# Weight sums ahead of the raw split, and seven-product pairs at places 1, 4 and 6, in a hybrid decoder layer

## The chip, the cores and the metric

The kernel runs on one core of a Trainium2 chip. The metric is the device time of one launch in microseconds (us), the median of several runs. Engines are named as in the profile: PE multiplies matrices (PEld is its weight load), DVE is the vector engine, ACT the scalar engine, POOL is GpSimd, and SP issues the DMAs of this kernel.

## The reference

One decoder layer for 256 tokens of width 2048 in float32: half a SwiGLU FFN, a token mixer of two head groups, and half an FFN again. Only the two FFNs are touched by the change.

```python
def swiglu(x, w_gate, w_up, w_down):
    return (jax.nn.silu(x @ w_gate) * (x @ w_up)) @ w_down

x = x + 0.5 * swiglu(rms_norm(x, ffn1_norm[l]), ffn1_w_gate[l], ffn1_w_up[l], ffn1_w_down[l])
...  # projection, attention, output projection
x = x + 0.5 * swiglu(rms_norm(x, ffn2_norm[l]), ffn2_w_gate[l], ffn2_w_up[l], ffn2_w_down[l])
```

`w_gate` and `w_up` are 2048 x 5632, `w_down` is 5632 x 2048.

## The kernel before

**Precision.** Each float32 operand is split into two parts, `hi` (a cast on ACT) and `lo` (the difference, on DVE), by `split`. A product is three matmuls of 128x512: hi by hi (L478), lo of x by hi of w (L479), hi of x by lo of w (L480).

**Pairs and blocks.** The width of an FFN, 5632, is cut into 11 chunks of 512. For a chunk, gate and up are computed together as a block product (`pair`); the down projection of one part (chunks 0 to 3, 4 to 7, 8 to 10) is computed for two column chunks at a time in the same way (`down`). Both call `blocks`, which goes over 8 places j (6 in the down projections of the last part). At each place a raw tile of 4 x 512 columns (`w_raw`, 1 MB, two DMAs) is loaded and multiplied. A **plain** place takes eight products (24 matmuls): its raw tile is cast whole (`w_hi`, `w_lo`, 128x2048). A **seven** place takes seven products by Strassen's scheme (21 matmuls): three quarters of the raw tile are split (128x1536), four sums of weights `w_t` are formed on DVE (L461, L463, L464) and split too (`t_hi`, `t_lo`). Which places are sevens is in `STRASSEN`; the last place is never one. Products are added up in PSUM banks m1 to m7. m1, m6 and m7 get products from sevens alone, so after the last seven place three operations (L487 to L489) turn them into `s1`, `v` and `u`, and at the end of the sequence more DVE operations put these together with m2 to m5.

There are 30 such sequences: 14 in FFN 1 (its first chunk and its last down projection are plain linear products) and 16 in FFN 2.

**Left-hand sides.** A seven needs other sums of x than a plain place: `Stage.put_sums` makes them for x, and `to_gT` for the activations g of a pair: two places per chunk, each with four transposes (L379), a copy, sums, and splits.

**Buffers and order.** `w_raw` has three buffers, `w_hi` and `w_lo` have two, `w_t`, `t_hi` and `t_lo` one. The four banks of one sequence's m2 to m5 are the other four for the next one (`banks.swap`): m2, m4 and m5 of the next sequence take the banks of m1, m6 and m7. The order in which each engine gets its instructions is set by a scheduler that reorders the program; an engine then executes its own list in that order, and a waiting instruction holds what is behind it.

Of the kernel before, what the change touches and what calls it, by code (L numbers as in the profile page):

```python
# [25 lines left out]
CH = 512  # L26
NCH = D_FF // CH
FF_PARTS = [(0, 4), (4, 8), (8, 11)]
STRASSEN = (1, 3, 5)
PAD_C, PAD_S, PAD_X = 256, 320, 224  # L30
CMP_BLOCK = 32
CMP_STRIDE = 16
# [13 lines left out]
def hybrid_layer(ctx: ExitStack, tc: tile.TileContext, d: dict, out: bass.AP):  # L46
# [146 lines left out]
    def split(hi, lo, src):  # L193
        cast = nc.scalar.copy(hi, src)  # L194
        nc.vector.tensor_tensor(lo, src, hi.bitcast(F32), op=ALU.subtract)  # L195
        return cast
# [40 lines left out]
    newest = {}  # L237
# [113 lines left out]
    def ffn(st, wg, wu, wd, after, fpool, last_part, plain_end, groups=None):  # L351
# [2 lines left out]
        wuv = wu.rearrange("(k p) n -> p k n", p=P)  # L354
        wdv = wd.rearrange("(k p) n -> p k n", p=P)

        def to_gT(slot, sg, odd, sums):


            yield from wait(2)  # L360
            hi = gpool.tile([P, 8, P], F32R, tag=f"ghi{slot}", name="ghi")
            lo = gpool.tile([P, 8, P], F32R, tag=f"glo{slot}", name="glo")
            xhi = fpool.tile([P, 5, P], F32R, tag=f"gxhi{slot}", name="gxhi")
            xlo = fpool.tile([P, 5, P], F32R, tag=f"gxlo{slot}", name="gxlo")

            def put(x, o, n, src):
                h, l = ((hi, lo), (xhi, xlo))[x]
                split(h[:, o:o + n], l[:, o:o + n], src)

            def where(x, o):  # L370
                h, l = ((hi, lo), (xhi, xlo))[x]
                return h[:, o], l[:, o]

            for i in range(2):
                seven = i == 1 and odd
                pt = misc("gt").rearrange("p (a b) -> p a b", b=P)
                order = ((0, 1), (0, 0), (1, 0), (1, 1)) if seven else ((0, 0), (0, 1), (1, 0), (1, 1))
                for n, (j, t) in enumerate(order):
                    nc.tensor.transpose(pt[:, n], sg[t][:, (2 * i + j) * P:(2 * i + j + 1) * P], ident)  # L379
                if not sums:  # L380
                    put(0, 4 * i, 4, pt)
                    g[2 * slot + i] = [where(0, 4 * i + f) for f in range(4)]
                    yield False
                    continue
                gf = fpool.tile([P, 8, P], F32, tag="sv", name="gf")
                nc.scalar.copy(gf[:, :4], pt)
                if seven:
                    put(1, 0, 3, pt[:, 1:])

                    nc.vector.tensor_tensor(gf[:, 4], gf[:, 0], gf[:, 1], op=ALU.subtract)  # L390
                    nc.vector.tensor_tensor(gf[:, 5:7], gf[:, 0:5:4], gf[:, 3:4].to_broadcast([P, 2, P]), op=ALU.add)
                    nc.vector.tensor_tensor(gf[:, 7], gf[:, 2], gf[:, 6], op=ALU.subtract)
                    put(0, 4, 4, gf[:, 4:])
                    g[2 * slot + 1] = {A11: where(1, 0), A12: where(1, 1), A22: where(1, 2), NS3: where(0, 4),
                                       S1: where(0, 5), S2: where(0, 6), S4: where(0, 7)}
                else:
                    put(0, 4 * i, 4, pt)
                    nc.vector.tensor_tensor(gf[:, 4:6], gf[:, 0:3:2], gf[:, 1:4:2], op=ALU.subtract)
                    o = 0 if i else 3
                    put(1, o, 2, gf[:, 4:6])  # L400
                    g[2 * slot + i] = {A11: where(0, 4 * i), A21: where(0, 4 * i + 1), A12: where(0, 4 * i + 2),
                                       A22: where(0, 4 * i + 3), S3: where(1, o), DD: where(1, o + 1)}
                yield False
# [30 lines left out]
        def blocks(nj, sevens, form, load, middle):  # L434

            pm = {i: acc(f"m{i}") for i in (2, 4, 5, 3)}
            side = banks.side
            banks.free = side[3:]  # L440
            seen = set()
            last = {}
            plan = []
            for j in range(nj):
                if j in sevens:

                    plan.append([(1, A11, 1), (2, A12, 2), (3, S4, 3), (5, S1, 4), (7, NS3, 5), (6, S2, 6), (4, A22, 7)])
                else:
                    plan.append([(2, A11, 1), (2, A12, 2), (4, A21, 1), (4, A22, 2), (5, A21, 0), (5, A22, 3),
                                 (3, S3, 0), (3, DD, 3)])  # L450
                for i, (m, _, _) in enumerate(plan[-1]):
                    last[m] = (j, i)
            for j in range(nj):
                raw = wpool.tile([P, 4, CH], F32, tag="raw", bufs=3, name="w_raw")
                newest["load"] = load(j, raw)
                whi = wpool.tile([P, 4, CH], F32R, tag="whi", name="w_hi")
                wlo = wpool.tile([P, 4, CH], F32R, tag="wlo", name="w_lo")
                if j in sevens:
                    newest["cast"] = split(whi[:, 1:4], wlo[:, 1:4], raw[:, 1:4])
                    ts = fpool.tile([P, 4, CH], F32, tag="ts", name="w_t")  # L460
                    nc.vector.tensor_tensor(ts[:, 0:2], raw[:, 0:1].to_broadcast([P, 2, CH]), raw[:, 1:4:2],  # L461
                                            op=ALU.subtract)
                    nc.vector.tensor_tensor(ts[:, 2], raw[:, 3], ts[:, 0], op=ALU.subtract)  # L463
                    nc.vector.tensor_tensor(ts[:, 3], raw[:, 2], ts[:, 2], op=ALU.subtract)  # L464
                    thi = fpool.tile([P, 4, CH], F32R, tag="thi", name="t_hi")
                    tlo = fpool.tile([P, 4, CH], F32R, tag="tlo", name="t_lo")
                    split(thi, tlo, ts)
                    for m in (1, 6, 7):
                        if m not in pm:
                            pm[m] = banks.tile(side[(1, 6, 7).index(m)], f"m{m}")  # L470
                else:
                    newest["cast"] = split(whi, wlo, raw)
                for i, (m, f, s) in enumerate(plan[j]):
                    ahi, alo = form(j, f)
                    bhi, blo = (whi[:, s], wlo[:, s]) if s < 4 else (thi[:, s - 4], tlo[:, s - 4])
                    first, end = m not in seen, last[m] == (j, i)
                    seen.add(m)
                    nc.tensor.matmul(pm[m], ahi, bhi, start=first, stop=False)  # L478
                    nc.tensor.matmul(pm[m], alo, bhi, start=False, stop=False)  # L479
                    nc.tensor.matmul(pm[m], ahi, blo, start=False, stop=end)  # L480
                    if i % 2 == 1:
                        pump()
                if j == max(sevens):

                    sv = fpool.tile([P, 2, CH], F32, tag="sv", name="sv")
                    s1, v, u = sv[:, 0], sv[:, 1], ev("u")
                    nc.scalar.copy(s1, pm[1])  # L487
                    nc.vector.tensor_tensor(v, pm[6], s1, op=ALU.add)
                    nc.vector.tensor_tensor(u, pm[7], v, op=ALU.add)  # L489
                    middle(s1, v, u)  # L490
            return pm, s1, v, u
# [26 lines left out]
        def down(k0, nj, ca, cb, ready):  # L518


            def load(j, raw):
                rows = slice(k0 + 2 * j, k0 + 2 * j + 2)
                nc.sync.dma_start(raw[:, 0:4:3], wdv[:, rows, cb * CH:(cb + 1) * CH])
                return nc.sync.dma_start(raw[:, 1:3], wdv[:, rows, ca * CH:(ca + 1) * CH]).ins

            def add(t, c, x):
                nc.vector.scalar_tensor_tensor(xr[t][c], x, 0.5, xr[t][c], op0=ALU.mult, op1=ALU.add)

            def middle(s1, v, u):
                add(0, ca, s1)  # L530
                add(0, cb, v)
                add(1, ca, u)
                add(1, cb, u)

            pm, s1, v, u = blocks(nj, [j for j in STRASSEN if j < nj - 1], gform, load, middle)
            add(0, ca, pm[2])
            add(1, ca, pm[4])
            if ready:
                ready(ca)
            add(0, cb, pm[5])  # L540
            add(1, cb, pm[5])
            add(0, cb, pm[3])
            banks.swap()
            if ready:
                ready(cb)

        for pi, (c0, c1) in enumerate(FF_PARTS):
# [4 lines left out]
            for c in range(c0, c1):  # L552
                sg = pair(c) if c else plain_pair(c)
                i = c - c0
                spawn(to_gT(i, sg, not plain and 2 * i + 1 in STRASSEN and 2 * i + 1 < nj - 1, not plain))
            if final:
                last_part()
            if not plain:
# [588 lines left out]
```

## Time and profile before

| | us |
|---|---|
| runs, median (lowest to highest of 3) | 1871.52 (1871.22 to 1871.9) |
| the profiled execution's own time | 1872.38 |
| its span | 1870.7 |
| PE busy | 1840.8 (98%) |
| PEld busy | 1509.9 (81%) |
| DVE busy | 1485.6 (79%) |
| ACT busy | 968.7 (52%) |

The busy time of PE is modelled, as matmuls overlap: a matmul of 128x512 is drawn 0.39 us long, and the next one may start 0.23 us after it. Idle time of an engine is listed with what ended it, which the profile infers from semaphores. Time of the engines other than the one at the bound costs nothing by itself.

### The profile page before, as it was taken

The numbers are of one execution on the slowest core, as the hardware profiler recorded it, in microseconds if no ns is written. First come the engines' busy times: TensorE is split into PE (matmuls) and PEld (weight loads), VectorE is DVE, ScalarE is ACT, GpSimd is POOL, SyncE is SP. The second block draws the span as 40 slices with busy tenths as digits, with TensorE's granted clock in tenths as the row PEclk, the third lists the DMA queues.
The fourth block names the chain that finished last, engine by engine and source line by source line (L and its number), as shares of the span: only waits on it lengthen the run. The fifth ranks groups of instructions, "written<-read, shape, count | busy, mean of one in ns | idle before, by whom it ended". The sixth has DMA issues, their size and how long they took to land.

```text
span 1870.7 us, 22225 instructions
## 1 busy us (share of the span) xinstructions
PE 1840.8 (98%) x8542; PEld 1509.9 (81%) x8542; DVE 1485.6 (79%) x1619; ACT 968.7 (52%) x1018; POOL 3.9 (0%) x22
## 2 busy tenths in 40 slices
PE   8999999999999999999999999999999999999998
PEld 6887788777788778788888888888788777788777
DVE  7888888888888875666655567788888888988887
ACT  7555444555454445335455555555544555545553
POOL 0000000000000000000000000000000000000000
PEclk9999999999999999999999999999999999999999
DMA  8655565655666655764533445655556555566554
GB/s 310 204 184 180 187 217 187 202 197 182 201 219 196 207 178 201 243 212 146 164 118 114 155 159 180 203 193 189 186 198 214 190 181 199 184 213 201 194 183 155
DMA packets 190762, 356.65 MB, mean 191 GB/s; under 512 B 10528, under 2 KB 25792, under 8 KB 190656
## 3 DMA queue, kind: packets, MB, share of 16 engines
q1 hardware_dynamic: 188912, 354.65, 57.3%
q8 instruction: 67, 1.10, 0.2%
q10 hardware_dynamic: 1744, 0.58, 0.1%
q14 instruction: 39, 0.32, 0.1%
HBM read 353.09 MB, written 2.10 MB: 190 GB/s over the span
## 4 chain that ended last, share of the span: by engine, by line
PE 93%; ACT 3%; DVE 2%; issue 1%; DMA 1%; SPq 0%; DVEq 0%; ACTq 0%
PE m L480 21%; PE m L478 21%; PE m L479 21%; PE in L258 4%; PE in L256 4%; PE in L257 4%; ACT t_hi L194 2%; PE wo L256 1%; PE wo L258 1%; PE wo L257 1%; PE down L258 1%; PE down L257 1%; PE down L256 1%; PE gt L379 1%; DVE w_lo L195 1%
## 5 line engine op out<-in xcount | busy, mean ns | idle before, releaser
L195 DVE TENSOR_TENSOR w_lo<-w_raw,w_hi 128x1536 fp32r<-128x1536 f32 (+3 forms) x331 | 694.0, 2101 | 209.9 <-ACT w_hi L194 195.5
L194 ACT CAST w_hi<-w_raw 128x1536 fp32r<-128x1536 f32 (+3 forms) x331 | 577.4, 1761 | 543.1 <-PE m L479 345.0
L478 PE MATMUL m<-w_hi,xhi 128*128 128x512 f32 x980 | 383.4, 391 | 2.1 <-ACT w_hi L194 2.1
L479 PE MATMUL m<-w_hi,xlo 128*128 128x512 f32 x980 | 381.9, 390 | 0.0
L480 PE MATMUL m<-w_lo,xhi 128*128 128x512 f32 x980 | 322.2, 391 | 2.3 <-DVE w_lo L195 2.3
L195 DVE TENSOR_TENSOR t_lo<-w_t,t_hi 128x2048 fp32r<-128x2048 f32 x88 | 201.2, 2287 | 48.8 <-ACT t_hi L194 48.7
L478 PEld LDWEIGHTS m<-w_hi,xhi 128*128 128x128 f32 x980 | 184.0, 188 | 44.8 <-ACT w_hi L194 7.3
L480 PEld LDWEIGHTS m<-w_lo,xhi 128*128 128x128 f32 x980 | 184.0, 188 | 41.5 <-DVE w_lo L195 3.1
L479 PEld LDWEIGHTS m<-w_hi,xlo 128*128 128x128 f32 x980 | 184.0, 188 | 37.8
L194 ACT CAST t_hi<-w_t 128x2048 fp32r<-128x2048 f32 x88 | 167.9, 1909 | 70.9 <-DVE w_t L464 68.0
L256 PE MATMUL in<-w_hi,xhi 128*128 128x512 f32 (+3 forms) x384 | 146.1, 381 | 0.0
L257 PE MATMUL in<-w_hi,xlo 128*128 128x512 f32 (+3 forms) x384 | 143.8, 375 | 0.0
L258 PE MATMUL in<-w_lo,xhi 128*128 128x512 f32 (+3 forms) x384 | 141.2, 379 | 1.0 <-DVE w_lo L195 0.9
L461 DVE TENSOR_TENSOR w_t<-w_raw 128x1024 f32<-128x1024 f32 x88 | 107.4, 1220 | 23.5 <-DMA w_raw<-in_ffn_w_gate 14.1
L478 PE MATMUL m<-w_hi,ghi 128*128 128x512 f32 x316 | 123.7, 392 | 1.9 <-ACT w_hi L194 1.8
L479 PE MATMUL m<-w_hi,glo 128*128 128x512 f32 x316 | 123.1, 390 | 0.0
L480 PE MATMUL m<-w_lo,ghi 128*128 128x512 f32 x316 | 109.9, 391 | 0.1
L478 PE MATMUL m<-t_hi,xhi 128*128 128x512 f32 x240 | 96.4, 402 | 7.9 <-ACT t_hi L194 7.9
L479 PE MATMUL m<-t_hi,xlo 128*128 128x512 f32 x240 | 94.0, 392 | 0.0
L256 PEld LDWEIGHTS in<-w_hi,xhi 128*128 128x128 f32 x384 | 72.3, 188 | 13.8 <-issue 3.1
L258 PEld LDWEIGHTS in<-w_lo,xhi 128*128 128x128 f32 x384 | 71.6, 188 | 14.3 <-DVE w_lo L195 2.1
L257 PEld LDWEIGHTS in<-w_hi,xlo 128*128 128x128 f32 x384 | 72.3, 188 | 10.6
(283 smaller groups left out, 2538.1 us busy)
## 6 DMA issues: line engine op xcount, KB each, us to landing
w_raw<-in_ffn_w_gate SPq DMA_DIRECT2D x163, 512.0 KB, 4.7
w_raw<-in_ffn_w_up SPq DMA_DIRECT2D x160, 512.0 KB, 3.8
w_raw<-in_ffn_w_down SPq DMA_DIRECT2D x152, 512.0 KB, 4.7
w_raw<-in_w_in SPq DMA_DIRECT2D x36, 1024.0 KB, 4.9
w_raw<-in_w_out SPq DMA_DIRECT2D x16, 1024.0 KB, 4.9
w_raw<-in_ffn_w_down SPq DMA_DIRECT2D x12, 1024.0 KB, 4.9
w_raw<-in_ffn_w_up SPq DMA_DIRECT2D x8, 1024.0 KB, 5.9
w_raw<-in_ffn_w_gate SPq DMA_DIRECT2D x6, 1024.0 KB, 5.1
```

The costliest lines, as they stand in the source:

```text
L194: cast = nc.scalar.copy(hi, src)
L195: nc.vector.tensor_tensor(lo, src, hi.bitcast(F32), op=ALU.subtract)
L256: nc.tensor.matmul(po[t][:, :n], xhi, whi[:, j], start=s, stop=False)
L257: nc.tensor.matmul(po[t][:, :n], xlo, whi[:, j], start=False, stop=False)
L258: nc.tensor.matmul(po[t][:, :n], xhi, wlo[:, j], start=False, stop=e)
L379: nc.tensor.transpose(pt[:, n], sg[t][:, (2 * i + j) * P:(2 * i + j + 1) * P], ident)
L461: nc.vector.tensor_tensor(ts[:, 0:2], raw[:, 0:1].to_broadcast([P, 2, CH]), raw[:, 1:4:2], op=ALU.subtract)
L478: nc.tensor.matmul(pm[m], ahi, bhi, start=first, stop=False)
L479: nc.tensor.matmul(pm[m], alo, bhi, start=False, stop=False)
L480: nc.tensor.matmul(pm[m], ahi, blo, start=False, stop=end)
```

## The change

Three things are changed, and the number of products, of DVE operations and of DMAs stays the same. The places of sevens become 1, 4 and 6 (1 and 4 where a sequence has six places). In `blocks` the three DVE operations that form `w_t` are written ahead of the split of the raw tile. `to_gT` can now make a seven's left-hand side for either place of a chunk (place 4 and 6 are the first of their chunks, where 1, 3 and 5 were the second).

```diff
-STRASSEN = (1, 3, 5)
+STRASSEN = (1, 4, 6)
...
+        def sevens(nj):
+            return [j for j in STRASSEN if j < nj - 1]
...
-                seven = i == 1 and odd
+                seven = 2 * slot + i in sevens
...
-                    put(0, 4, 4, gf[:, 4:])
-                    g[2 * slot + 1] = {A11: where(1, 0), A12: where(1, 1), A22: where(1, 2), NS3: where(0, 4),
-                                       S1: where(0, 5), S2: where(0, 6), S4: where(0, 7)}
+                    put(0, 4 * i, 4, gf[:, 4:])
+                    g[2 * slot + i] = {A11: where(1, 0), A12: where(1, 1), A22: where(1, 2), NS3: where(0, 4 * i),
+                                       S1: where(0, 4 * i + 1), S2: where(0, 4 * i + 2), S4: where(0, 4 * i + 3)}
...
-                    o = 0 if i else 3
+                    o = 0 if i and 2 * slot not in sevens else 3
...
                 if j in sevens:
-                    newest["cast"] = split(whi[:, 1:4], wlo[:, 1:4], raw[:, 1:4])
                     ts = fpool.tile([P, 4, CH], F32, tag="ts", name="w_t")
                     nc.vector.tensor_tensor(ts[:, 0:2], raw[:, 0:1].to_broadcast([P, 2, CH]), raw[:, 1:4:2],
                                             op=ALU.subtract)
                     nc.vector.tensor_tensor(ts[:, 2], raw[:, 3], ts[:, 0], op=ALU.subtract)
                     nc.vector.tensor_tensor(ts[:, 3], raw[:, 2], ts[:, 2], op=ALU.subtract)
+                    newest["cast"] = split(whi[:, 1:4], wlo[:, 1:4], raw[:, 1:4])
...
-            pm, s1, v, u = blocks(nj, [j for j in STRASSEN if j < nj - 1], gform, load, middle)
+            pm, s1, v, u = blocks(nj, sevens(nj), gform, load, middle)
```

Since a scheduler sets the order, the rows of the engines show the change better than the diff. All of the following rows are from the gate-and-up pair of chunk 5 in FFN 1 (the profile's stretch from 319 to 363 us). Lines are numbered three higher in the changed kernel.

On ACT, before: `w_hi_2583`, `w_hi_2614`, `w_hi_2655` and `w_hi_2686` are the casts of places 4, 5 (a seven), 6 and 7; `t_hi_2622` is the cast of place 5's weight sums; gf, gxhi and ghi belong to `to_gT`.

```order
L194 CAST w_hi_2583<-w_raw_2580 128x2048
L194 CAST w_hi_2614<-w_raw_2611 128x1536
L386 COPY gf_2459<-gt_2454 128x512
L194 CAST gxhi_2434<-gt_2454 128x384
L194 CAST w_hi_2655<-w_raw_2652 128x2048
L194 CAST t_hi_2622<-w_t_2618 128x2048
L194 CAST ghi_2432<-gf_2459 128x512
L194 CAST w_hi_2686<-w_raw_2683 128x2048
```

On ACT, of the change: `w_hi_2578`, `w_hi_2614`, `w_hi_2645` and `w_hi_2686` are places 4 (a seven), 5, 6 (a seven) and 7; `t_hi_2586` and `t_hi_2653` are the weight sums of places 4 and 6.

```order
L194 CAST w_hi_2578<-w_raw_2575 128x1536
L194 CAST t_hi_2586<-w_t_2580 128x2048
L389 COPY gf_2459<-gt_2454 128x512
L194 CAST gxhi_2434<-gt_2454 128x384
L194 CAST w_hi_2614<-w_raw_2611 128x2048
L194 CAST w_hi_2645<-w_raw_2642 128x1536
L194 CAST ghi_2432<-gf_2459 128x512
L194 CAST t_hi_2653<-w_t_2647 128x2048
L194 CAST w_hi_2686<-w_raw_2683 128x2048
```

Before, the cast of a seven's sums stands behind the cast of the next place's raw tile; now it stands behind the cast of its own place.

On PE, before: the last reads of `w_hi_2583` (place 4) and the first of `w_hi_2655` (place 6), which goes into the same buffer.

```order
L479 MATMUL m3_2412<-w_hi_2583,xlo4_265 128x512
L480 MATMUL m3_2412<-w_lo_2584,xhi4_264 128x512
L478 MATMUL m2_2409<-w_hi_2614,xhi5_298 128x512
L479 MATMUL m2_2409<-w_hi_2614,xlo5_299 128x512
L478 MATMUL m3_2412<-w_hi_2614,xhi5_298 128x512
L479 MATMUL m3_2412<-w_hi_2614,xlo5_299 128x512
L480 MATMUL m1_2489<-w_lo_2615,xhi5_298 128x512
L480 MATMUL m2_2409<-w_lo_2615,xhi5_298 128x512
L480 MATMUL m3_2412<-w_lo_2615,xhi5_298 128x512
L478 MATMUL m2_2409<-w_hi_2655,xhi6_324 128x512
```

On PE, of the change: the last read of `w_hi_2578` (place 4) and what follows. Behind these rows stand four of `t_lo_2587` and eight of `w_hi_2614` (place 5), and then the first read of `w_hi_2645` (place 6), which takes the buffer of `w_hi_2578`.

```order
L482 MATMUL m3_2412<-w_hi_2578,xlo4_265 128x512
L483 MATMUL m1_2489<-w_lo_2579,xhi4_264 128x512
L483 MATMUL m2_2409<-w_lo_2579,xhi4_264 128x512
L483 MATMUL m3_2412<-w_lo_2579,xhi4_264 128x512
L481 MATMUL m5_2411<-t_hi_2586,xhi4_264 128x512
L482 MATMUL m5_2411<-t_hi_2586,xlo4_265 128x512
L481 MATMUL m7_2491<-t_hi_2586,xhi4_264 128x512
L482 MATMUL m7_2491<-t_hi_2586,xlo4_265 128x512
L481 MATMUL m6_2490<-t_hi_2586,xhi4_264 128x512
L482 MATMUL m6_2490<-t_hi_2586,xlo4_265 128x512
L481 MATMUL m4_2410<-t_hi_2586,xhi4_264 128x512
L482 MATMUL m4_2410<-t_hi_2586,xlo4_265 128x512
```

Before, the first read of the next tile in that buffer is the 9th row behind the last read of the old one; now it is the 24th.

On DVE, before, at the end of that pair: places 6 and 7 of the pair (`w_lo_2656`, `w_lo_2687`), places 0 and 1 of the next (`w_lo_2733`, `w_t_2797`, `t_lo_2802`), and between them `v` (L488), `u` (L489) and the operations of the pair's end (L506 to L510).

```order
L195 TENSOR_TENSOR w_lo_2656<-w_raw_2652,w_hi_2655 128x2048
L195 TENSOR_TENSOR t_lo_2623<-w_t_2618,t_hi_2622 128x2048
L195 TENSOR_TENSOR glo_2433<-gf_2459,ghi_2432 128x512
L195 TENSOR_TENSOR w_lo_2687<-w_raw_2683,w_hi_2686 128x2048
L461 TENSOR_TENSOR w_t_2797<-w_raw_2790 128x1024
L488 TENSOR_TENSOR sv_2647<-m6_2490,sv_2647 128x512
L463 TENSOR_TENSOR w_t_2797<-w_raw_2790,w_t_2797 128x512
L489 TENSOR_TENSOR u_2648<-m7_2491,sv_2647 128x512
L464 TENSOR_TENSOR w_t_2797<-w_raw_2790,w_t_2797 128x512
L506 TENSOR_TENSOR g0_2714<-m2_2409,sv_2647 128x512
L195 TENSOR_TENSOR w_lo_2733<-w_raw_2729,w_hi_2732 128x2048
L508 TENSOR_TENSOR g1_2715<-m4_2410,u_2648 128x512
```

On DVE, of the change, the same place: 6 is a seven now (`w_lo_2646`, `t_lo_2654`), `w_lo_2687` is place 7, `w_lo_2733` place 0 and `w_t_2793` place 1 of the next pair.

```order
L195 TENSOR_TENSOR w_lo_2646<-w_raw_2642,w_hi_2645 128x1536
L195 TENSOR_TENSOR glo_2433<-gf_2459,ghi_2432 128x512
L195 TENSOR_TENSOR t_lo_2654<-w_t_2647,t_hi_2653 128x2048
L463 TENSOR_TENSOR w_t_2793<-w_raw_2788 128x1024
L195 TENSOR_TENSOR w_lo_2687<-w_raw_2683,w_hi_2686 128x2048
L465 TENSOR_TENSOR w_t_2793<-w_raw_2788,w_t_2793 128x512
L195 TENSOR_TENSOR w_lo_2733<-w_raw_2729,w_hi_2732 128x2048
L491 TENSOR_TENSOR sv_2678<-m6_2490,sv_2678 128x512
L466 TENSOR_TENSOR w_t_2793<-w_raw_2788,w_t_2793 128x512
L509 TENSOR_TENSOR g0_2714<-m2_2409,sv_2678 128x512
L492 TENSOR_TENSOR u_2679<-m7_2491,sv_2678 128x512
L511 TENSOR_TENSOR g1_2715<-m4_2410,u_2679 128x512
```

The first sum of the next pair's seven moved ahead of the split of place 7, and `v` and `u` moved behind the splits of place 7 and of the next pair's place 0.

## Rows read from the trace of the kernel before

**Rows 1.** The page, part 1: busy time, share of the span, instructions.

```profile
PE 1840.8 (98%) x8542; PEld 1509.9 (81%) x8542; DVE 1485.6 (79%) x1619; ACT 968.7 (52%) x1018; POOL 3.9 (0%) x22
```

**Rows 2.** What PE waited for: us in total, times, longest us.

```profile
PE m L478 <- ACT t_hi L194: 10.8, 18, 0.6
PE m L478 <- ACT w_hi L194: 3.8, 17, 0.7
...
PE m L480 <- DVE w_lo L195: 2.3, 2, 1.1
...
PE down L256 <- ACT w_hi L194: 0.9, 1, 0.9
...
PE down L258 <- DVE w_lo L195: 0.7, 1, 0.7
```

**Rows 3.** Timeline of PE in chunk 5: start us, us, instruction, idle before it.

```profile
340.43 0.39 PE L479 MATMUL m<-w_hi,xlo 128*128 128x512 f32 x1
...
341.79 0.84 PE L480 MATMUL m<-w_lo,xhi 128*128 128x512 f32 x3
342.82 0.50 PE L478 MATMUL m<-w_hi,xhi 128*128 128x512 f32 x1 [0.19 <-ACT w_hi L194]
...
344.62 0.50 PE L478 MATMUL m<-t_hi,xhi 128*128 128x512 f32 x1 [0.60 <-ACT t_hi L194]
...
346.57 0.39 PE L480 MATMUL m<-w_lo,xhi 128*128 128x512 f32 x1
...
349.30 1.07 PE L480 MATMUL m<-t_lo,xhi 128*128 128x512 f32 x4
350.21 0.39 PE L478 MATMUL m<-w_hi,xhi 128*128 128x512 f32 x1
```

**Rows 4.** Timeline of ACT in the same stretch.

```profile
333.88 0.48 ACT L194 CAST gxhi<-gt 128x384 fp32r<-128x384 f32 x1
340.86 1.91 ACT L194 CAST w_hi<-w_raw 128x2048 fp32r<-128x2048 f32 x1 [6.49 <-PE m L479]
342.67 1.90 ACT L194 CAST t_hi<-w_t 128x2048 fp32r<-128x2048 f32 x1
```

**Rows 5.** Timeline of DVE in the same stretch.

```profile
337.97 0.68 DVE L463 TENSOR_TENSOR w_t<-w_raw,w_t 128x512 f32<-128x512 f32 x1
338.57 0.42 DVE L391 TENSOR_TENSOR gf<-gf 128x256 f32<-128x256 f32 x1
338.90 0.69 DVE L464 TENSOR_TENSOR w_t<-w_raw,w_t 128x512 f32<-128x512 f32 x1
...
342.80 2.29 DVE L195 TENSOR_TENSOR w_lo<-w_raw,w_hi 128x2048 fp32r<-128x2048 f32 x1 [3.01 <-ACT w_hi L194]
345.01 2.28 DVE L195 TENSOR_TENSOR t_lo<-w_t,t_hi 128x2048 fp32r<-128x2048 f32 x1
347.21 0.69 DVE L195 TENSOR_TENSOR glo<-gf,ghi 128x512 fp32r<-128x512 f32 x1
...
350.33 1.23 DVE L461 TENSOR_TENSOR w_t<-w_raw 128x1024 f32<-128x1024 f32 x1 [0.23 <-DMA w_raw<-in_ffn_w_gate]
351.48 0.68 DVE L488 TENSOR_TENSOR sv<-m,sv 128x512 f32<-128x512 f32 x1
```

**Rows 6.** The chain that ended last: start us, us, what; one landmark in successive pairs.

```profile
119.19 0.91 PE m L480 x4
...
161.66 0.91 PE m L480 x4
...
366.92 0.91 PE m L480 x4
...
410.80 0.91 PE m L480 x4
```

**Rows 7.** Stretches of 47 us: PE, PEld, DVE, ACT, POOL busy (x), clock, DMA share, GB/s.

```profile
94.00:141.00 47.00, 47.00 (x212) 38.88 (x211) 41.83 (x40) 24.83 (x22) 0.00 (x0) 1.00 0.55 180
...
423.00:470.00 47.00, 46.21 (x207) 37.58 (x206) 41.73 (x42) 24.34 (x21) 0.00 (x0) 1.00 0.60 195
```

More of the change, by code (lines that the diff above doesn't have):

```diff
@@ L355, in ffn, with to_gT @@
         wdv = wd.rearrange("(k p) n -> p k n", p=P)
-        def to_gT(slot, sg, odd, sums):
+        def sevens(nj):
+            return [j for j in STRASSEN if j < nj - 1]
+        def to_gT(slot, sg, sevens, sums):
             yield from wait(2)
@@ L554, in ffn @@
                 i = c - c0
-                spawn(to_gT(i, sg, not plain and 2 * i + 1 in STRASSEN and 2 * i + 1 < nj - 1, not plain))
+                spawn(to_gT(i, sg, () if plain else sevens(nj), not plain))
             if final:
```

## The prediction

> **What bounds the kernel now.** I read the page's busy times first: PE 98% of the span, DVE 79%, ACT 52%, POOL nothing [rows 1]. PE does the same matmuls after the change, so only its stalls can go. But 98% is no measure of how little that is, because a busy PE is drawn with overlapping matmuls. The second view is therefore what PE waited for [rows 2]: in the block products 10.8 us for the casts of weight sums (`t_hi`, 18 times), 3.8 us for casts of raw tiles (`w_hi`, 17 times) and 2.3 us for `w_lo` (twice), 16.9 us in 37 waits. Two more waits, 0.9 and 0.7 us, are in plain linear products (L256, L258).
>
> The third view is the timeline of one such place. Four matmuls take 350.21 - 349.30 = 0.91 us, 0.227 us each, when nothing is waited for. From 341.79 to 346.57 there are 15 of them, 3.40 us of work in 4.78 us [rows 3]. So the two waits there cost 1.38 us, though their printed idle is only 0.19 + 0.60 = 0.79: the rest, 0.30 us a wait, is drawn as busy. The chain of what ended last confirms it. One landmark in successive pairs is 43.88 us apart in a stretch with the stall (366.92 to 410.80) and 42.47 us in one without (119.19 to 161.66), 1.41 us apart [rows 6]. The engine that the wait names is ACT, and the timeline of ACT tells why: it idles 6.49 us until PE's last read of the old tile at 340.43, casts `w_hi` from 340.86, and only then, at 342.67, `t_hi` [rows 4]. The sums that `t_hi` needs were done at 338.90 + 0.69 = 339.59 [rows 5], so that cast waits for nothing but its place in ACT's queue.
>
> **What the order asks of PE.** After the last read at 340.43, PE can take the new `w_hi` at 342.82, 2.39 us or 10.5 matmuls later, and the `t_hi` behind it at 344.62, 4.19 us or 18.5 matmuls later [rows 3]. A sequence stalls where PE has fewer matmuls than that to do in between. In the order of before there are 9 from the last read of `w_hi` to the first read of its successor in 16 of the 30 sequences, 10 to 13 at the tightest place of the others. That agrees with the 17 and 18 waits.
>
> **The change part by part.**
>
> *Places and the written order, in the pairs and down projections.* A plain place that follows a seven gives 24 matmuls of cover; a seven that follows a plain place starts with the parts of its own raw tile. In the new order the smallest distance from a last read of `w_hi` to the first read of its successor is 12 matmuls once (place 2 of the last sequence), 17 in twelve sequences, and 19 or more elsewhere, against 10.5 needed. `t_hi` now stands behind the cast of its own place's tile, whose buffer came free early, or directly behind the copies of `to_gT`. Its first read comes 32 matmuls or more after the buffer's release, against 18.5. `w_lo` has 27 or more, where the stalled ones had 12 to 22. So all 37 waits go: 16.9 + 37 x 0.30 = **-28.0 us**. As a check from the other side, 18 stalled sequences at 1.38 are 24.8, and the two waits for `w_lo` 2.3 + 0.6, together 27.7.
>
> The Trainium skill, in "Perfetto Trace Analysis", section "Identifying the Most-Contended Engine", says that matmul busy time is a poor measure of how near TensorE is to its limit and that the busy share of weight loads is a better one. The trace bears that out: between a stretch without stalls and one with them, PE loses 0.79 us of 47 by its own busy time, but PEld goes from 38.88 to 37.58, 3.3%, which is 1.57 us in 47 [rows 7]. By the idle column alone the gain would be 16.9 us and the time about 1856; by the rule, as by the landmarks, it is the 28.
>
> *The sums ahead of the split, on DVE.* Nothing is added: the same operations, other order. One 512-wide sum takes 338.57 - 337.97 = 0.60 us from start to start, a 2048-wide split 347.21 - 345.01 = 2.20, the first sum, of 1024, 1.15 [rows 5]. The split of the raw tile comes up to 1.15 + 2 x 0.60 = 2.35 us later than before relative to its cast. In a seven PE first takes eight matmuls of `w_hi` or more before it reads `w_lo`, and DVE had idled 3.01 us ahead of a split [rows 5]. Within a sequence I price this at nothing; the cover is the 27 matmuls (6.1 us) between release and first read of `w_lo`; without it one such wait would be up to 1.4 us, as in [rows 3].
>
> *The end of a sequence, where the cover is thin.* With sevens at 1, 3 and 5 two plain places stood behind the last seven; now one does, 24 matmuls or 5.45 us. In it, and in place 0 of the next sequence, DVE must split places 7 and 0, form `v` and `u`, evacuate, and make the next seven's sums. I walked DVE's order with the durations above, with time zero at PE's first product of place 7. The first sum of the next pair waits for a raw tile: its DMA lands 5.24 us after the `w_lo` before it was done with the buffer (345.09 to 350.33) [rows 5], at -3.1. Behind it `w_lo` of place 7 runs from -2.0 to 0.2, needed at 2.7; `w_lo` of place 0 to 3.0, needed at 6.4; `v` to 3.6, needed at 8.2 when PE wants the bank of m6; the next `t_hi` to 6.0, needed at 10.9; `u` to 5.4, needed at 9.5. The least slack is 2.5 us, taken with up to 1 us of error in the walk as 1.5. In pairs I price it at nothing. From a down projection to the next one (4 boundaries), nine additions crowd DVE and the slack falls to 0.5 to 0.85 us. There I allow 0 to 1 us each. In the last part's pair before the final down projection, the new place 4's left-hand side is behind a cast on ACT and comes up to 1.5 us late, where a wait of 1.1 stood before (the longest for `w_lo`) [rows 2]. For both I take **+1.5 us**, between 0 and 5.5.
>
> *Outside the block products.* FFN 1's last plain down projection waits 0.9 + 0.7 us now [rows 2], 2.2 us with 0.30 for each. The new order puts its first products among those of the pair before it, which may take these waits away: 0 to -2.2, taken as 0. The mixer's order is almost unchanged, and the last additions end as they did. The granted clock is 1.00 in both stretches of [rows 7], the higher level (2.4 GHz), and PE has only less idle time, so I expect no change of it.
>
> **Sum.** 1872.4 - 28.0 + 1.5 = 1845.9 us for a profiled execution; the median of the runs is 0.9 us under the profiled one, so the forecast is **1845 us**.
>
> **The rivals.**
>
> *Waits that stay or move.* `w_hi` still has two buffers, `t_hi` one, and places 4 and 6 are two apart like 3 and 5. If the casts still end last, each pair has its 1.4 us in another place, and the time is **1871**. For it speaks that ACT's wait is for a buffer [rows 4]. Against it: the `t_hi` wait is three quarters of the pair's printed loss, and it was only the queue. The Trainium skill, in "Perfetto Trace Analysis", section "Optimization Strategy", says that the same gap repeating on the engine that should be saturated can mean that SBUF or PSUM is too small for the next tile, buffer counts among it. By that rule an order alone brings nothing and the time is that of this rival; the trace agrees for the `w_hi` cast, which waits for PE's last read, and disagrees for `t_hi`. Chance 0.08. In between is a partial gain: waits stay in about half of the 30 sequences, or at all down boundaries, 14 us less gain, **1858**; chance 0.13.
>
> *The boundary becomes the bound (slower).* DVE is busy 41.83 of 47 us where nothing stalls, 89% [rows 7], with all of its slack now at the end of a sequence. The place is the first sum of the next pair, which waits for a DMA and holds the split of place 7, place 0's split, `v` and `u` behind it on DVE; before, that sum already waited for its raw tile, 0.23 us, with only `v` and `u` behind it [rows 5]. It decides from the point at which that tile lands more than 2.4 us later than walked. The DMA share is 0.55 to 0.60 [rows 7], so transfers aren't saturated, which speaks against it. If each of the 30 boundaries then costs a double wait like that of [rows 3], it is 30 x 1.38 = 41.4 us against the 26.5 gained: **1886**. Chance 0.09.
>
> **How the numbers follow.** Forecast 0.70, partial gain 0.13, same 0.08, slower 0.09. The low end is the sum with nothing lost at boundaries and the linear waits gone, 1845 - 1.5 - 2.2 = 1841. Upwards the bounds of the boundary terms reach 1849, and the range goes on over the partial gain to 1859; what is left out is the same, the slower and a little at either end. A measurement of this kernel can tell about 0.2%, 3.7 us, from no change: faster 0.83 (forecast and partial gain), same 0.08, slower 0.09.
>
> **What would show it.** PE's waits for `t_hi` and `w_hi` in block products fall from 14.6 us to under 3; the landmark comes every 42.5 us in all pairs of an FFN; PEld is near 38.9 in every 47 us of block products. ACT still idles until PE's last read ahead of `w_hi`, which no longer matters, and DVE waits for a DMA at the first sum of a pair. The forecast is wrong if PE waits for `w_lo`, or for `v` and `u` through the banks m4 and m5, at the starts of sequences, or if ACT's `t_hi` shows again at places 4 and 6.

## The result and the profile after

The changed kernel takes 1844.57 us (median) against 1871.71 for the kernel before: ratio 0.9854, 95% interval 0.9839 to 0.9869. The forecast was 1845. The profiled execution takes 1843.87 us, its span is 1841.8. One of the four executions of the changed kernel took 2628.22 us at a mean granted clock of 0.654; the ratio is that of the other three.

The page of the changed kernel, part 1 (busy time, share, instructions), answers to [rows 1]:

```profile
PE 1828.4 (99%) x8542; PEld 1513.4 (82%) x8542; DVE 1489.3 (81%) x1619; ACT 973.0 (53%) x1018; POOL 3.9 (0%) x22
```

What PE waited for in it (us in total, times, longest), answering to [rows 2]. L481 to L483 are the three matmuls of the block products now:

```profile
PE gate L256 <- ACT w_hi L194: 4.3, 2, 3.8
...
PE m L481 <- ACT gxhi L194: 1.1, 1, 1.1
...
PE m L483 <- DVE w_lo L195: 0.5, 1, 0.5
```

Of 16.9 us in 37 waits, 1.6 us in two are left, and the waits of the plain down projection (L256, L258 `down`) are gone. Busy time in the two stretches of [rows 7] (PE, PEld, DVE, ACT, POOL, clock, DMA share, GB/s) is now alike:

```profile
94.00:141.00 47.00, 47.00 (x213) 38.88 (x212) 42.31 (x42) 24.55 (x21) 0.00 (x0) 1.00 0.63 207
423.00:470.00 47.00, 47.00 (x213) 38.88 (x212) 41.01 (x39) 25.61 (x21) 0.00 (x0) 1.00 0.62 211
```

In the second one PEld was 37.58 before. The clock stays at the higher level (1.00).

The pair of chunk 5, timeline of PE (start, us, instruction): the first product of place 6's weight sums, its last ones, the first of place 7 and its first `w_lo`, and the same `t_lo` landmark two pairs on:

```profile
342.48 0.39 PE L481 MATMUL m<-t_hi,xhi 128*128 128x512 f32 x1
...
344.30 1.07 PE L483 MATMUL m<-t_lo,xhi 128*128 128x512 f32 x4
345.20 0.39 PE L481 MATMUL m<-w_hi,xhi 128*128 128x512 f32 x1
...
347.92 0.39 PE L483 MATMUL m<-w_lo,xhi 128*128 128x512 f32 x1
...
429.24 1.07 PE L483 MATMUL m<-t_lo,xhi 128*128 128x512 f32 x4
```

From 344.30 to 429.24 are 84.94 us, twice the 42.47 that [rows 6] gave for a pair without a stall. The timeline of ACT there:

```profile
325.72 1.90 ACT L194 CAST t_hi<-w_t 128x2048 fp32r<-128x2048 f32 x1
...
335.83 1.92 ACT L194 CAST t_hi<-w_t 128x2048 fp32r<-128x2048 f32 x1
340.91 3.72 ACT L194 CAST w_hi<-w_raw 128x2048 fp32r<-128x2048 f32 x2 [3.17 <-PE m L482]
...
351.14 1.92 ACT L194 CAST t_hi<-w_t 128x2048 fp32r<-128x2048 f32 x1 [6.04 <-DVE w_t L466]
```

ACT still waits for PE's last read ahead of `w_hi` (3.17 us), as forecast, but `t_hi` of place 6 is done at 337.75, 4.7 us before PE reads it. The timeline of DVE there, at the end of the pair (L466 is the last sum of a seven; the 1536-wide splits are those of the raw tiles of places 4 and 6):

```profile
325.85 1.76 DVE L195 TENSOR_TENSOR w_lo<-w_raw,w_hi 128x1536 fp32r<-128x1536 f32 x1 [0.41 <-ACT w_hi L194]
...
335.03 0.69 DVE L466 TENSOR_TENSOR w_t<-w_raw,w_t 128x512 f32<-128x512 f32 x1
335.63 1.75 DVE L195 TENSOR_TENSOR w_lo<-w_raw,w_hi 128x1536 fp32r<-128x1536 f32 x1
...
343.60 1.22 DVE L463 TENSOR_TENSOR w_t<-w_raw 128x1024 f32<-128x1024 f32 x1 [3.42 <-DMA w_raw<-in_ffn_w_gate]
344.75 2.28 DVE L195 TENSOR_TENSOR w_lo<-w_raw,w_hi 128x2048 fp32r<-128x2048 f32 x1
...
349.75 0.68 DVE L491 TENSOR_TENSOR sv<-m,sv 128x512 f32<-128x512 f32 x1
...
351.55 0.68 DVE L492 TENSOR_TENSOR u<-m,sv 128x512 f32<-128x512 f32 x1
```

The first sum of the next pair waits for a transfer, and place 7's split stands behind it. It ends at 347.03, and PE reads it at 347.92: 0.9 us of slack, where the walk had 2.5.

### The profile page after: what moved, and what is told of

Read it like the earlier page. It is cut to its first block, busy times and chain, and to the rows that moved or that the text cites. A ratio compares the mean times of both kernels' runs of the same rounds, so it can differ in the third digit from the quotient of the medians.

```text
span 1841.8 us, 22229 instructions
## 1 busy us (share of the span) xinstructions
PE 1828.4 (99%) x8542; PEld 1513.4 (82%) x8542; DVE 1489.3 (81%) x1619; ACT 973.0 (53%) x1018; POOL 3.9 (0%) x22
## 4 chain that ended last, share of the span: by engine, by line
PE 97%; DVE 1%; issue 1%; ACT 0%; DMA 0%; DVEq 0%; SPq 0%
PE m L481 22%; PE m L483 22%; PE m L482 22%; PE in L258 4%; PE in L256 4%; PE in L257 4%; PE wo L256 1%; PE wo L258 1%; PE wo L257 1%; PE down L258 1%; PE down L256 1%; PE down L257 1%; PE gt L382 1%; PE no L953 1%; PE gate L258 1%; PE gate L256 1%
## 5 line engine op out<-in xcount | busy, mean ns | idle before, releaser
L195 DVE TENSOR_TENSOR w_lo<-w_raw,w_hi 128x2048 fp32r<-128x2048 f32 (+3 forms) x331 | 694.1, 2100 | 186.3 <-ACT w_hi L194 181.4
L194 ACT CAST w_hi<-w_raw 128x2048 fp32r<-128x2048 f32 (+3 forms) x331 | 578.0, 1762 | 433.8 <-PE m L482 240.4
L481 PE MATMUL m<-w_hi,xhi 128*128 128x512 f32 x980 | 381.8, 390 | 0.0
L483 PE MATMUL m<-w_lo,xhi 128*128 128x512 f32 x980 | 320.9, 392 | 0.5 <-DVE w_lo L195 0.5
L483 PEld LDWEIGHTS m<-w_lo,xhi 128*128 128x128 f32 x980 | 183.7, 188 | 38.8 <-DVE w_lo L195 1.3
L481 PEld LDWEIGHTS m<-w_hi,xhi 128*128 128x128 f32 x980 | 184.0, 188 | 37.7
L256 PE MATMUL in<-w_hi,xhi 128*128 128x512 f32 (+3 forms) x384 | 146.1, 381 | 0.0
L258 PE MATMUL in<-w_lo,xhi 128*128 128x512 f32 (+3 forms) x384 | 141.2, 379 | 1.1 <-DVE w_lo L195 1.1
L481 PE MATMUL m<-w_hi,ghi 128*128 128x512 f32 x316 | 122.7, 389 | 0.0
L483 PE MATMUL m<-w_lo,ghi 128*128 128x512 f32 x316 | 111.5, 391 | 0.0
L481 PE MATMUL m<-t_hi,xhi 128*128 128x512 f32 x240 | 93.2, 389 | 0.0
L256 PEld LDWEIGHTS in<-w_hi,xhi 128*128 128x128 f32 x384 | 72.3, 188 | 13.8 <-issue 3.1
L258 PEld LDWEIGHTS in<-w_lo,xhi 128*128 128x128 f32 x384 | 71.7, 188 | 14.4 <-DVE w_lo L195 2.3
```

What stands on the lines that cost most here:

```text
L256: nc.tensor.matmul(po[t][:, :n], xhi, whi[:, j], start=s, stop=False)
L258: nc.tensor.matmul(po[t][:, :n], xhi, wlo[:, j], start=False, stop=e)
```

## The experiments

Ratios are to runs of the kernel before on the same chip, with 95% intervals.

**1. The two halves apart.** The changed kernel with the split written ahead of the sums again, and the kernel before with the sums ahead of the split:

```diff
+                    newest["cast"] = split(whi[:, 1:4], wlo[:, 1:4], raw[:, 1:4])
                     ts = fpool.tile([P, 4, CH], F32, tag="ts", name="w_t")
...
-                    newest["cast"] = split(whi[:, 1:4], wlo[:, 1:4], raw[:, 1:4])
```

> The places 1, 4 and 6 without the sums written ahead of the split. In the order that the scheduler makes of it, no engine's list differs from that of the changed kernel, since the scheduler had put the sums ahead of the split by itself. Theory (the places alone do it): 1844.6 us, ratio 0.985 of the kernel before, PE's waits in block products as in the changed kernel (1.6 us in 2). Rival (the written order carries part of the gain): 1850 to 1865 us.

Measured: 1845.07 us, 0.9855 (0.9840 to 0.9869).

> The sums written ahead of the split, places 1, 3 and 5 as before. No engine's list differs from that of the kernel before. Theory: no change, 1871.7 us, ratio 1.000 within 0.001, and the same 18 waits for t_hi and 17 for w_hi. Rival (the written order carries part of the gain): 5 to 20 us faster.

Measured: 1872.27 us, 0.9999 (0.9990 to 1.0008). In both cases the instruction lists of PE, DVE, ACT and SP don't differ by a row from those without the edit. Both theories came true: the whole gain is that of the places, and the written order of sums and split is undone by the scheduler. That doesn't make the order on DVE indifferent. With the new places the scheduler puts place 6's split behind its sums (335.03, then 335.63 above); at 1, 3 and 5 it puts a seven's split between them (379.47 and 382.74 in experiment 2). No run holds that order by itself.

**2. Only the order on ACT.** My reading of [rows 4] was that the stall of `t_hi` was its place in ACT's queue. This run mends that and leaves the places:

```diff
-                    split(thi, tlo, ts)
+                    tcast = split(thi, tlo, ts).ins
...
-                    newest["cast"] = split(whi, wlo, raw)
+                    if j - 1 in sevens:
+                        with tc.issue_after(tcast):
+                            newest["cast"] = split(whi, wlo, raw)
+                    else:
+                        newest["cast"] = split(whi, wlo, raw)
```

> The kernel before, places 1, 3 and 5, with one thing added: on ACT the raw cast of a plain place behind a seven may not be issued ahead of the seven's t_hi cast. The scheduler then also puts PE's first products of that plain place behind those of t_hi: the smallest distance from the last read of a w_hi buffer to the first read of its successor becomes 16 matmuls, where 10.5 are needed. Theory (the stall was the order on ACT's queue, and what PE had between release and first read): the 37 waits go as with the changed places, 1844 to 1850 us. Rival 1 (places two apart with two w_hi buffers are the cause): the w_hi waits stay, 18 x 0.5 = 9 us of the 28 remain, and t_hi goes, 1854 us or more. Rival 2 (the gain belongs to the places alone): 1866 to 1872 us.

Measured: 1873.32 us, 1.0004 (0.9994 to 1.0013). None of the three came true as put: the `w_hi` waits are gone, but the time is no shorter; rival 2 came nearest, 1.3 us under the measured time. PE's waits:

```profile
PE m L482 <- ACT t_hi L194: 18.9, 18, 2.0
```

Besides these there are two for `w_lo`, 1.5 us. The `t_hi` waits became longer. Where they come from shows in the pair of chunk 6, from one seven (place 3) to the next (place 5). PE, ACT and DVE:

```profile
373.95 0.50 PE L482 MATMUL m<-t_hi,xhi 128*128 128x512 f32 x1 [0.46 <-ACT t_hi L194]
...
385.50 0.50 PE L482 MATMUL m<-t_hi,xhi 128*128 128x512 f32 x1 [1.03 <-ACT t_hi L194]
```

```profile
371.99 1.91 ACT L194 CAST t_hi<-w_t 128x2048 fp32r<-128x2048 f32 x1 [0.84 <-DVE w_t L464]
...
383.54 1.91 ACT L194 CAST t_hi<-w_t 128x2048 fp32r<-128x2048 f32 x1 [5.59 <-DVE w_t L464]
```

```profile
373.93 2.29 DVE L195 TENSOR_TENSOR t_lo<-w_t,t_hi 128x2048 fp32r<-128x2048 f32 x1 [1.69 <-ACT t_hi L194]
376.13 2.28 DVE L195 TENSOR_TENSOR w_lo<-w_raw,w_hi 128x2048 fp32r<-128x2048 f32 x1
378.34 1.22 DVE L461 TENSOR_TENSOR w_t<-w_raw 128x1024 f32<-128x1024 f32 x1
379.47 1.75 DVE L195 TENSOR_TENSOR w_lo<-w_raw,w_hi 128x1536 fp32r<-128x1536 f32 x1
...
382.74 0.69 DVE L464 TENSOR_TENSOR w_t<-w_raw,w_t 128x512 f32<-128x512 f32 x1
```

There is a chain: `t_hi` on ACT, then on DVE `t_lo`, the split of the plain place, the split and the sums of the next seven, then its `t_hi`. It takes 383.54 - 371.99 = 11.55 us. PE needs 45 matmuls for the two places, 45 x 0.227 = 10.2 us. So the chain falls some 1.3 us behind PE at every seven that stands two places behind another, and PE waits unless the chain had a lead. The kernel before, in its pair of chunk 6, takes as long: from place 3's `t_hi` at 371.66 to the end of place 5's sums at 382.76 + 0.68 = 383.44 are 11.8 us. In the changed kernel the same distance, place 4 to 6, is 335.83 - 325.72 = 10.1 us, and the lead at its end is 4.7 us. There a seven's split stands behind its sums: place 4's runs while its `t_hi` is cast (from 325.85), and place 6's comes after the chain (335.63). In run queue DVE idles 1.69 us for the cast, and place 5's split stands in the chain with 1.67 us (379.47 to 381.14, where DVE's next instruction starts).

**3. Less work in that chain.** Places 1, 3 and 5 again, with the order held as in run 2 and without. Both kernels leave out half of `w_lo` at places 2 and 4; the number of matmuls stays the same:

```diff
+                short = j - 1 in sevens and j + 1 in sevens
...
-                        newest["cast"] = split(whi, wlo, raw)
+                        newest["cast"] = split_short(whi, wlo, raw, short)
...
+        nc.vector.tensor_tensor(lo[:, :2], src[:, :2], hi[:, :2].bitcast(F32), op=ALU.subtract)
...
-                    bhi, blo = (whi[:, s], wlo[:, s]) if s < 4 else (thi[:, s - 4], tlo[:, s - 4])
+                    bhi, blo = (whi[:, s], wlo[:, s % 2 if short else s]) if s < 4 else (thi[:, s - 4], tlo[:, s - 4])
```

> The kernel of the run queue (places 1, 3 and 5, t_hi held ahead of the next raw cast on ACT) with 1.1 us of DVE work less at each plain place between two sevens: places 2 and 4 split only half of their raw tile, and PE uses that half twice, so that half of w_lo is left out of the products of those places. No w_hi buffer has under 10.5 matmuls, as in queue. Theory after queue (with sevens at 1, 3 and 5 the chain on DVE and ACT from one seven's t_hi to the next one's, t_lo, w_lo, w_t, t_hi, takes 11.55 us in queue where PE needs 10.2 us for the two places, and the lag adds up): most of the 18 waits of 18.9 us go, 1846 to 1852 us. Rival (the held order on ACT itself delays the casts, or the places are at fault whatever DVE does): no change from queue, 1868 to 1873 us.

Measured: 1841.03 us, 0.9834 (0.9819 to 0.9848), 5 us under the theory's range. PE's waits in the whole launch:

```profile
PE gate L263 <- ACT w_hi L194: 3.0, 2, 2.3
PE idle L119 <- DVE idle L116: 1.3, 1, 1.3
PE in L265 <- DVE w_lo L195: 0.9, 2, 0.5
PE wo L263 <- ACT w_hi L194: 0.7, 1, 0.7
```

> The kernel before with the same half of w_lo left out at places 2 and 4, and no order held by hand. With that load the scheduler itself puts t_hi ahead of the next raw cast: no place has under 10.5 matmuls for w_hi or under 18.5 for a t_hi behind it. Theory (DVE's load between sevens that stand two apart is the cause; the order on ACT and PE follows from it): 1844 to 1850 us. Rival (ACT's order alone): the same by its order, so that this run only tells whether the scheduler's order follows from DVE's load. Rival (the two w_hi buffers are the cause): 1855 us or more.

Measured: 1841.10 us, 0.9835 (0.9818 to 0.9851), 3 us under the range, and no wait in block products either. With 1.1 us less for DVE between two sevens, places 1, 3 and 5 have no stalls. But the two kernels are no two orders: in their traces the instruction lists of PE, DVE, ACT and SP are the same, row for row. The scheduler makes of the lighter load by itself what run queue_lo holds, and its order of before, with its 9 matmuls, isn't made any more. So run before_lo doesn't separate order from load. From run queue to queue_lo the held order is the same in both and the load goes down, and the time goes from 1873 to 1841; but the scheduler moves other instructions there too, so this step isn't the load alone. What the trace shows is the chain itself, ACT and PE in the pair of chunk 6 of queue_lo:

```profile
365.25 1.92 ACT L194 CAST t_hi<-w_t 128x2048 fp32r<-128x2048 f32 x1
...
375.73 1.91 ACT L194 CAST t_hi<-w_t 128x2048 fp32r<-128x2048 f32 x1 [3.35 <-DVE w_t L472]
```

```profile
380.50 0.39 PE L490 MATMUL m<-t_hi,xhi 128*128 128x512 f32 x1
```

It takes 10.48 us instead of 11.55, the 1.1 us that the split gave back, and `t_hi` is done at 377.64, 2.9 us before PE reads it.

**4. Other places.** In each only `STRASSEN` of the changed kernel is replaced, by the three numbers of the label.

```diff
-STRASSEN = (1, 4, 6)
+STRASSEN = (1, 3, 6)
```

> The changed kernel with sevens at 1, 3 and 6. By the order, place 4 has 9 matmuls between the release of its w_hi buffer and its first read in 9 sequences, with the t_hi of place 3 behind it on ACT at 13, and 10 to 15 in 5 more. Theory (a wait is where PE has fewer than 10.5 matmuls for w_hi or 18.5 for the t_hi behind it): 9 x 1.38 + 5 x 1.1 = 18 us above the changed kernel, 1862 us, with 14 waits for t_hi and 9 to 13 for w_hi at places 3 and 4. Rival (any set that is not 1, 3, 5 frees DVE or ACT as well as 1, 4, 6): 1845 us. Rival (two plain places behind a seven cost nothing, only the end of a sequence counts): 1845 to 1848 us.

Measured: 1859.06 us, 0.9929 (0.9913 to 0.9946), 3 us under the theory; both rivals fell.

```profile
PE m L481 <- ACT t_hi L194: 9.1, 15, 0.6
...
PE m L481 <- ACT w_hi L194: 1.7, 9, 0.2
```

The 9 waits for `w_hi` are those of the nine sequences with 9 matmuls, and 14 of the 15 for `t_hi` were listed by the order. 10.8 us printed and 24 x 0.30 make 18.0; the span is 15.7 over that of the changed kernel, which has 2.2 us of its own waits by the same count.

> The changed kernel with sevens at 2, 4 and 6. By its order, t_hi stands behind a raw cast with 13 matmuls in 6 sequences and 16.5 in 4, and w_hi has 8 to 10 matmuls in 14 further places. Theory (a wait is where PE has fewer than 10.5 matmuls for w_hi or 18.5 for a t_hi behind it): 6 x 1.38 + 4 x 0.6 + 7 x 0.5 + 7 x 0.25 = 16 us above the changed kernel, 1858 to 1863 us. Rival (one plain place behind the last seven instead of two is what helps): 1845 us.

Measured: 1865.76 us, 0.9966 (0.9953 to 0.9979), 3 us over the range.

```profile
PE m L481 <- ACT t_hi L194: 4.2, 10, 0.6
...
PE m L481 <- ACT w_hi L194: 3.9, 14, 0.6
```

The 10 waits for `t_hi` and the 14 for `w_hi` came as counted; three for `w_lo` (2.2 us), one of 1.2 us for `glo` and the old waits of the plain down projection came besides.

> The changed kernel with sevens at 0, 3 and 5: going round from one sequence to the next the distances between sevens are 3, 2 and 3 places, as with 1, 4 and 6 (where they are 3, 2, 3 as well); 1, 3 and 5 has 2, 2 and 4. No place has under 10.5 matmuls for w_hi or 18.5 for a t_hi behind it by the order. Theory (sevens spread evenly give DVE the time between them, and then no distance is short): 1841 to 1848 us, under 4 us of waits in block products. Rival (it is the one plain place at the end of a sequence that 1, 4 and 6 has): with two at the end, waits as before, 1860 us or more.

Measured: 1844.91 us, 0.9854 (0.9840 to 0.9869), the time of the changed kernel.

```profile
PE m L483 <- DVE w_lo L195: 1.7, 3, 1.0
```

> The changed kernel with sevens at 1, 2 and 5: distances 1, 3 and 4 places, the least even. The order has one place of 10 matmuls for w_hi and none under 18.5 for a t_hi. If the distances in the order are the whole cause: 1843 to 1847 us. If what counts is the chain on DVE and ACT from one seven's t_hi to the next one's (t_lo 2.2, w_lo 1.7, sums and cast behind it) against PE's 4.8 us between two neighbours: PE waits for t_hi at place 2 in most of the 30 sequences, 0.5 to 1.4 us each, 1855 to 1885 us.

Measured: 1879.08 us, 1.0038 (1.0024 to 1.0052).

```profile
PE m L481 <- ACT t_hi L194: 9.4, 14, 1.1
PE m L483 <- DVE w_lo L195: 9.0, 13, 1.5
```

This separates two kinds of wait. The order has next to no short distance at 1, 2 and 5, and the kernel is slower than before. Distances in the order tell where a wait shows when a cast is ready to run and stands in ACT's queue; the chain of DVE and ACT between two sevens tells whether the sums are there in time. The traces tell the two apart by the time from the end of a seven's sums to the start of its `t_hi` cast, ahead of each wait of PE for `t_hi`. It is 1.5 to 3.3 us in the kernel before (all 18 waits), 2.3 to 3.1 in run p246 (all 10) and 1.3 to 2.5 in run p136 (14 of 15): there the cast stood in the queue. It is 0.1 to 0.9 us in run queue (all 18) and under 0.8 in run s125 (13 of 14): there the sums came late.

With 2, 2 and 4 places from seven to seven (1, 3, 5 and 2, 4, 6) there are waits, with 1, 3 and 4 more, with 3, 2 and 3 (1, 4, 6 and 0, 3, 5) next to none. That isn't the whole rule: 1, 3 and 6 has the distances 2, 3 and 3 as well, and waits. Ahead of one of these waits, in a pair of FFN 1, DVE and ACT:

```profile
326.77 0.69 DVE L466 TENSOR_TENSOR w_t<-w_raw,w_t 128x512 f32<-128x512 f32 x1
```

```profile
327.80 1.91 ACT L194 CAST w_hi<-w_raw 128x2048 fp32r<-128x2048 f32 x1 [1.09 <-PE m L482]
329.62 1.90 ACT L194 CAST t_hi<-w_t 128x2048 fp32r<-128x2048 f32 x1
```

The sums were done at 327.46, and the cast stood behind a `w_hi` cast that waited for PE. What 1, 3 and 6 takes with the order held on ACT was not tried; whether the chain would then be late there too, as at 1, 3 and 5, is open.

**5. What DVE can carry.** Four sevens, and the sums on the idle POOL:

```diff
-STRASSEN = (1, 4, 6)
+STRASSEN = (1, 3, 4, 6)
...
-    cpool.tile([P, PAD_C // 4], F32, tag="pad", name="pad_c")
-    spool.tile([P, PAD_S // 4], F32, tag="pad", bufs=1, name="pad_s")
```

> The changed kernel with four sevens, at 1, 3, 4 and 6 (1, 3 and 4 where a sequence has six places), to see what DVE can carry; the two padding tiles are left out to make room. PE saves 30 x 3 matmuls, 20.4 us; DVE gets about 4 us more a sequence, 37.8 + 4.0 = 41.8 us of work against the 41.8 us that PE needs. Theory (DVE's work between sevens bounds their number and their spacing): PE waits for t_hi and w_lo in most sequences, and the time is 1870 to 1910 us. Rival (DVE's 19% of idle time is free to use): 1824 to 1835 us.

Measured: 1991.39 us, 1.0636 (1.0614 to 1.0657), far over the range.

```profile
PE m L479 <- ACT t_hi L192: 39.5, 49, 2.4
PE m L479 <- ACT w_hi L192: 36.0, 24, 3.8
```

DVE's idle time was no free time here; the sum of its work against PE's (41.8 to 41.8) did not tell the size of the loss. The mean granted clock of this execution was 0.989, against 0.999 in the changed kernel, so some 20 us of the 147 (an estimate, 1% of the time) can be the clock.

```diff
-                    nc.vector.tensor_tensor(ts[:, 2], raw[:, 3], ts[:, 0], op=ALU.subtract)
+                    nc.gpsimd.tensor_tensor(ts[:, 2], raw[:, 3], ts[:, 0], op=ALU.subtract)
```

(and so for the two other sums)

> The changed kernel with the three sums of each seven (w_t) on POOL instead of DVE; 2.35 us less on DVE for each seven, 7 us a sequence. No run shows a POOL operation of this size. Theory (DVE's load between sevens sets the waits, and only 1.6 us of them are left): 1841 to 1845 us if POOL forms the sums of one seven in under 8 us and DVE is not slowed. Rival (POOL is too slow or slows DVE down): t_hi comes late in every seven and the time is 1860 us or far more.

Measured: 2005.82 us, 1.0709 (1.0678 to 1.0740). On POOL the three sums take 3.36, 1.96 and 1.59 us in the mean, 6.9 together, under the 8 I had asked for. The other condition, that DVE isn't slowed, failed: its 2048-wide splits of raw tiles take 2.48 us in the mean, against 2.29 in the changed kernel. What ACT and PE waited for:

```profile
ACT t_hi L194 <- POOL w_t L466: 370.2, 69, 8.1
```

```profile
PE m L481 <- ACT w_hi L194: 61.6, 39, 3.3
```

> Four sevens, at 1, 3, 4 and 6, with the sums on POOL. DVE falls from 41.8 to 32.4 us a sequence, PE needs 41.8 us. Theory (DVE's load is the limit in the run f1346): the waits of 95 us mostly go and the time is 1824 to 1840 us, if POOL carries four times three sums in 41.8 us, under 10 us a seven, and doesn't slow DVE. Rival (POOL takes longer, or the two compete): 1860 us or more, with PE waiting for t_hi and ACT for w_t.

Measured: 2116.24 us, 1.1298 (1.1266 to 1.1331). The rival's time holds in both runs, its mechanism as put in the second: there PE waits 131.3 us for `t_hi` (75 times) and ACT 379.5 for POOL's last sum. In run pool_after ACT waits for POOL as well, but of PE's waits only 8.6 us are for `t_hi`. Most are for `w_hi`; in one pair of the trace that cast, at 341.30, stands behind a `t_hi` cast at 338.86 that had waited 7.38 us for POOL. No version beat the changed kernel while computing the whole.

## Why the prediction was right, and where it was not

**What bounds the kernel, and the price of a wait.** Right. 16.9 us printed plus 0.30 for each of 37 waits is 28.0; the profiled execution became 28.5 us shorter. By the idle column alone it would have been 1856. The 0.30 also fits run p136 (18.0 against 15.7 + 2.2). In the runs queue and s125 the same count stays some 3 us short (26.4 against 27.6 + 2.2, 35.0 against 35.3 + 2.2); for queue the last section shows a part of the rest.

**Distances in the order.** Right as a description: where the order left fewer than 10.5 or 18.5 matmuls, waits came, in before, p136 and p246, and there the cast did stand in ACT's queue. Wrong as the whole cause. "That cast waits for nothing but its place in ACT's queue" is true of that moment, and the step from it to a gain of 28 us is the one that failed: run queue gave `t_hi` its place and won nothing. The sums that were done at 339.59 [rows 5] were in time in that pair, as I read it, because PE had been held back in the pairs before; with those stalls gone the chain from seven to seven (11.55 us against 10.2) makes them late. I had priced the work between sevens on DVE at nothing and looked at DVE at the boundary alone. That the forecast came true all the same is in part luck: by the same reading run queue was to take 1844 to 1850 us, and it took 1873. The new places relieve the chain as well, which the prediction had not asked for: most sevens get three places of time, and at the distance of two that is left the split stands outside the chain. How much each of these two brings was not separated.

**Sums ahead of the split.** The cost was rightly nothing, for a wrong reason: not a cover hides a later split, but the edit makes no split later. The list of DVE is the same with either text; where the sums do stand ahead of the split, as at place 6, that comes with the places.

**The end of a sequence.** Rightly without a wait in pairs, with the slack mis-sized. With time zero at 345.20, place 7's split ended at 1.8 (walked: 0.2), `v` at 5.2 (3.6), `u` at 7.0 (5.4), the next `t_hi` at 7.9 (6.0). All are 1.6 to 1.9 us late. Of that, 1.0 us is the raw tile, which was there 6.2 us after `w_lo` of place 6 (337.38 to 343.60) instead of 5.24; another 0.5 is that this `w_lo` ended later than walked. The term of +1.5 came out as 1.1 + 0.5 us printed, 2.2 with 0.30 each: for the left-hand side `gxhi` of the last part, as forecast, and for `w_lo` at the start of a pair, not from one down projection to the next. The 1.1 us that the prediction took from [rows 2] for the last pair belongs elsewhere: the two waits of that length stand far ahead of the last pairs, at 171.66 in FFN 1 and at 1312.55 in FFN 2. The first of them in the kernel before:

```profile
171.66 0.50 PE L480 MATMUL m<-w_lo,xhi 128*128 128x512 f32 x1 [1.13 <-DVE w_lo L195]
```

**Outside the block products.** The 2.2 us of the plain down projection, taken as 0 with a bound of -2.2, were regained. The prediction left out the other waits of plain products; of these the ones at the start of the kernel cost 0.6 more (`gate`, 3.7 to 4.3). So the sum is -28.0 + 2.2 - 2.2 + 0.6 = -27.4 against -28.5 measured; 1.1 us is left without a name.

**The rivals.** "Waits stay or move" fell for this change, but it describes what run queue did. The Trainium skill ("Perfetto Trace Analysis", section "Optimization Strategy") says that the same gap repeating can mean too few buffers. Here more buffers were not needed: with the same two `w_hi` buffers the gaps are gone in the changed kernel, at 0, 3 and 5, and at 1, 3 and 5 with less work on DVE. What a third buffer would do was not tried. The slower rival, DVE at the boundary, did not come true, but by less than walked: place 7's split was done 0.9 us ahead of PE, not 2.5.

## What to carry to other kernels

A wait names the engine that came last, and that engine's queue shows why in that place. Whether another order mends it depends on the whole chain that has to come round between two such places, so hold its length against what the bound engine does in that time. Here a queue order alone won nothing, and spreading the heavy places more evenly won 27 us. And where a scheduler sets the order, compare the instruction lists before pricing an edit of the text, and before calling two kernels two orders.

## What the runs showed of the hardware

A wait can cost more than its idle time and the 0.30 us. In run queue PE waited 2.02 us four times. Behind two of these waits (ending at 213.71 and 1613.33) the granted clock fell to the lower level for some 3.4 us (0.57 in the mean of 4 us); behind the other two it stayed at 1.00. One of each (us, then PE, PEld, DVE, ACT, POOL, clock, DMA share, GB/s):

```profile
214.00:218.00 4.00, 4.00 (x12) 3.08 (x12) 4.00 (x2) 3.26 (x2) 0.00 (x0) 0.57 0.42 160
475.00:479.00 4.00, 3.89 (x17) 3.18 (x18) 3.91 (x2) 3.68 (x3) 0.00 (x0) 1.00 0.48 179
```

In the first PE starts 12 matmuls in the 4 us, in the second 17, so each such stretch costs about 1 us more (an estimate from the five missing ones at 0.227).

POOL and DVE hold each other up. In run pool_after, timelines of POOL and DVE:

```profile
330.69 3.46 POOL L463 TENSOR_TENSOR w_t<-w_raw 128x1024 f32<-128x1024 f32 x1 [5.26 <-DMA w_raw<-in_ffn_w_gate]
334.24 3.23 POOL L465 TENSOR_TENSOR w_t<-w_raw,w_t 128x512 f32<-128x512 f32 x1
337.54 1.29 POOL L466 TENSOR_TENSOR w_t<-w_raw,w_t 128x512 f32<-128x512 f32 x1
```

```profile
332.42 3.89 DVE L195 TENSOR_TENSOR w_lo<-w_raw,w_hi 128x2048 fp32r<-128x2048 f32 x1
```

The split that takes 2.29 us elsewhere takes 3.89: it is issued while POOL works until 334.15, and ends 2.16 us after that. POOL's 512-wide sum, 1.29 us when alone, then takes 3.23 and ends 1.16 us after DVE's split. The Trainium skill ("SBUF — State Buffer", section "SBUF: two separate sides") says that a GpSimd operation and a DVE operation with two inputs in SBUF hold their shared ports in turn, each for its whole instruction; this trace agrees.
